# Cross attention's turned keys and weights at other places, and a counter moved where four stages begin

## The chip, the cores and the metric

The kernel runs on one NeuronCore of a Trainium2 chip. TensorE (PE, with its weight loads PEld), VectorE (DVE), ScalarE (ACT), GpSimd (POOL) and SyncE (SP) each work through a queue of their own and wait for each other by semaphores. The metric is the device time of one execution, in microseconds; the times shown are those of several executions, and one more was profiled.

## The reference, cut to what matters

One step of a decoder layer, for two groups that share weights: a prompt of 1024 rows, and eight sample rows that each attend to 8192 cached tokens in pages.

```python
q, k, v, logf, u, z = mixer_inputs(rmsnorm(xp, g_mix), w_in, b_f, g_sgu_v)        # prompt
xp = xp + merge_heads(fox_prompt(q, k, v, logf), sgu_prompt(u, z, w_s, b_s), g_att_out, g_sgu_out, w_o)
mk, mv = memory_kv(mem_prompt, g_mem, w_ck, w_cv)
xp = xp + cross_attend(rmsnorm(xp, g_cross), mk, mv, w_cq, w_co)
f, conv_p = conv_ffn(rmsnorm(xp, g_ffn), zeros, w_up, conv_w, conv_b, w_down);  xp = xp + f
q, k, v, logf, u, z = mixer_inputs(rmsnorm(xs, g_mix), w_in, b_f, g_sgu_v)        # sample: the same layer,
att = fox_sample(q, k, v, logf, cache_k, cache_v, cache_logf, page_table)         # attention over the cache

def cross_attend(xn, mk, mv, w_cq, w_co):        # 4 heads of 256, 256 memory tokens
    q = (xn @ w_cq).reshape(B, T, MEM_HEADS, MEM_HEAD_DIM)
    s = jnp.einsum('bqhd,bmhd->bhqm', q, mk) * (MEM_HEAD_DIM ** -0.5)
    p = jax.nn.softmax(s, axis=-1)
    o = jnp.einsum('bhqm,bmhd->bqhd', p, mv).reshape(B, T, MEM_HEADS * MEM_HEAD_DIM)
    return o @ w_co
```

Outputs are both groups behind a final norm, and the new keys, values, gates and convolution states.

## The kernel before, in words

The prompt is worked through in two halves of 512 rows, as a chain of stages whose names stand in `phase[0]`: `p1` (the input projection), `att0` and `attx` (attention of half 0), `att1` (attention of half 1), `mid0` (merge, output projection and cross attention of half 0), `ffn0`, `mid1`, `ffn1`. Projections are made of three products each (`gemm3`, L272 to L274, or the loops at L1062 to L1064), from weights that SP loads (L249) and ScalarE and VectorE split into a high and a low part (L235, L236).

Cross attention, `cross` (L1137), works on four heads. Its pieces are

- `fetch(h)`: SP loads the head's keys (L1143) and values (L1145);
- `keys(h)`: four transposes on PE (L1170) and a copy on ScalarE (L1174) turn the keys;
- `weigh(h)`: 16 score products in the trace (L1187), a maximum on VectorE (L1189), its scaling (L1192), the exponential (L1195), the reciprocal of the sum on VectorE (L1198), and the scaling of the weights on ScalarE (L1200);
- `turned(h)`: eight transposes (L1207) and two copies (L1208) turn the weights;
- `gather(h)`: the output products (L1215), split by ScalarE and VectorE (L235, L236).

Before these come the query projections, two times four products of 24, in a loop over `n` and `dt_`; `keys(0)`, `keys(1)`, `weigh(0)` and `weigh(1)` stand inside that loop. Behind them stands the output projection. Accumulators in PSUM rotate: four tiles `ba` and two `bb` (`BK`), and the projections, transposes, scores and outputs all draw from these six. Small tiles `t` (seven buffers) hold keys and values.

The sample's work, `sample` (decode, L1371 and on, then `sample_rest`), runs beside the prompt as a list of steps. Each of the 128 key steps gathers four tokens of each half page of cached keys by an indirect DMA that POOL issues (L1425) into one of four tiles `kv`, multiplies by the query and sums on VectorE (L1441 and L1445, in the attention stages L1432 and L1433); value steps gather values (L1486) into the same tiles, in pairs, and PE makes the products (L1492).

What sets the order is a counter. The prompt is a generator that yields its work in units (5.2 for a projection of 24 products, 1 to 4 for a piece of cross attention). Each yield is added to `acc[0]`; while the counter holds at least `PACE` of the stage, a step of the sample's generator is issued and the pace subtracted. In the attention stages a key step is cut into five pieces of 0.2. `held[0]` stops steps between the last output projection of a stage and the end of the next norm; the counter runs on, and the steps are caught up behind it, not more than one yield's worth and one at a time. Once the decode is done, `phase[1]` is `rest` and its pace counts.

The order in which all this is written isn't the last word: `kernel` asks for a planner that lays the written instructions out on a timeline of its own (`schedule_with_timeline_sim`), and gives each engine its queue from that. Some instructions are tied behind others by hand (`behind`, `issue_after`).

Of the kernel before, what the change touches and what calls it, by code (L numbers as in the profile page):

```python
# [73 lines left out]
BKQ = 1  # L74
LA = (2, 2)
PACE = {'p1': 7.0, 'att0': 12.0, 'attx': 26.0, 'mid0': 8.0, 'ffn0': 8.5, 'att1': 11.0, 'mid1': 6.8, 'ffn1': 2.5, 'rest': 2.9}


def build(nc, tc, ctx, a, phases=None):
# [31 lines left out]
    def U(shape, dt=F32):  # L111
        n = 1
        for s in shape[1:]:
            n *= s
        t = upool.tile([P, UW], dt, tag="u", bufs=NU, name=nm("u"))[:, :n]
        if len(shape) == 3:
            t = t.rearrange("p (a b) -> p a b", b=shape[2])
        return t

    def T2(n=512, dt=F32):  # L120
        return tpool.tile([P, 512], dt, tag="t2", bufs=NT, name=nm("t2"))[:, :n]
# [24 lines left out]
    def BK():  # L146
        turn_[0] += 1
        return BB() if turn_[0] % BR == BR - 1 else BA()
# [83 lines left out]
    def split(src, h, l, scale=None):  # L232

        if scale is None:
            nc.scalar.activation(h, src, AF.Copy)  # L235
            nc.vector.tensor_tensor(l, src, h.bitcast(F32), op=ALU.subtract)  # L236
        else:
            nc.scalar.activation(h, src, AF.Copy, scale=scale)
            nc.vector.scalar_tensor_tensor(l, src, scale, h.bitcast(F32), op0=ALU.mult, op1=ALU.subtract)  # L239
# [897 lines left out]
    def cross(xt, sq):  # L1137
        mkn, mkT, mv, pp, pT = ([None] * MH for _ in range(5))

        def fetch(h):  # L1140
            hc = slice(h * MD, (h + 1) * MD)
            mkn[h] = T2().rearrange("p (a b) -> p a b", b=256)
            nc.sync.dma_start(mkn[h], mk_d[:, hc].rearrange("(a p) b -> p a b", p=P))  # L1143
            mv[h] = T2().rearrange("p (a b) -> p a b", b=256)
            nc.sync.dma_start(mv[h], mv_d[:, hc].rearrange("(a p) b -> p a b", p=P))  # L1145
# [20 lines left out]
        def keys(h):  # L1166
            tr = TR()
            for dd in range(2):
                for mt in range(2):
                    nc.tensor.transpose(  # L1170
                        tr[:, dd * 256 + mt * P : dd * 256 + (mt + 1) * P], mkn[h][:, mt, dd * P : (dd + 1) * P], ident
                    )
            mkT[h] = T2().rearrange("p (a b) -> p a b", b=256)
            nc.scalar.activation(mkT[h], tr.rearrange("p (a b) -> p a b", b=256), AF.Copy)  # L1174
# [27 lines left out]
        def turned(h):  # L1202
            pT[h] = U([P, 2, 512])
            for mt in range(2):
                tr = TR()
                for i in range(4):
                    nc.tensor.transpose(tr[:, i * P : (i + 1) * P], pp[h][:, i, mt * P : (mt + 1) * P], ident)  # L1207
                nc.scalar.activation(pT[h][:, mt, :], tr, AF.Copy)  # L1208

        def gather(h):  # L1210
            oh2, ol2 = U([P, 2, 512], F32R), U([P, 2, 512], F32R)
            for dd in range(2):
                ps = BK()
                for mt in range(2):
                    mmul(ps, mv[h][:, mt, dd * P : (dd + 1) * P], pT[h][:, mt, :], start=(mt == 0), stop=(mt == 1))  # L1215
                split(ps, oh2[:, dd, :], ol2[:, dd, :])
                oh.append(oh2[:, dd, :])
                ol.append(ol2[:, dd, :])
# [3 lines left out]
        for n in range(2):  # L1222
            if n:
                ws = [wload(wpair(a["wt_cq"], kk, n * 512, 512), 1024) for kk in range(4)]
            for dt_ in range(4):
# [12 lines left out]
                    fetch(2)  # L1238
                if n and 1 <= dt_ < 3:
                    weigh(dt_ - 1)  # L1240
        keys(2)
        fetch(3)
        turned(0)
        yield 1
        weigh(2)
        yield 3
        gather(0)
        yield 4
        keys(3)
        turned(1)  # L1250
        yield 1
        weigh(3)
        yield 3
        gather(1)
        yield 4
        for h in (2, 3):
            turned(h)
            yield 1
            gather(h)
            yield 4  # L1260
        ys = []
        sq = yield from out_proj(a["wt_co"], oh, ol, xt, ys=ys)
        return ys
# [100 lines left out]
    bgs, acc, phase = [], [0.0], ["p1", None]  # L1364
# [547 lines left out]
    def sample():  # L1912
        yield from decode()
        phase[1] = "rest"
        yield from sample_rest()


    bgs.append(sample())
    seen = 0
    for t in prompt():  # L1920
        ins = nc.cur_bb.bb.instructions
        for e in (ENG.DVE, ENG.PE):
            for i in range(len(ins) - 1, max(seen, len(ins) - 400) - 1, -1):
                if ins[i].engine == e:
                    last[e] = ins[i]
                    break
        if paused[0]:
            t = 0.0
        acc[0] += t
        most = int(t / PACE[phase[1] or phase[0]]) + 1  # L1930
        while bgs and not held[0] and most and acc[0] >= PACE[phase[1] or phase[0]]:
            most -= 1
            acc[0] -= PACE[phase[1] or phase[0]]
            w = next(bgs[0], None)
            if w is None:
                bgs.pop()
            else:
                acc[0] -= (w - 1) * PACE[phase[1] or phase[0]]
        seen = len(nc.cur_bb.bb.instructions)
# [100 lines left out]
```

## Time and profile before

| | us |
|---|---|
| median of 3 runs (lowest to highest) | 1791.92 (1788.94 to 1793.47) |
| the profiled execution | 1793.48 |
| its span | 1791.6 |
| PE busy | 1734.9 (97%) |
| DVE busy | 1401.0 (78%) |
| ACT busy | 733.6 (41%) |
| POOL busy | 483.6 (27%) |

Its mean granted TensorE clock is 0.993 of full speed. By stages, cut at times read from the trace, PE is busy

| stretch, us | stage | PE busy, us | PE idle, us | granted clock |
|---|---|---|---|---|
| 0 to 290 | p1 | 282.25 | 7.75 | 1.00 |
| 290 to 480 | att0, attx, att1 | 169.57 | 20.43 | 0.98 |
| 480 to 694 | mid0 | 208.26 | 5.74 | 0.98 |
| 694 to 1090 | ffn0 | 390.69 | 5.31 | 0.99 |
| 1090 to 1337 | mid1 | 239.79 | 7.21 | 1.00 |
| 1337 to 1791 | ffn1 | 444.34 | 9.66 | 0.99 |

In a row of the order of time stand the start in us, the length in us, the engine, the line, the operation, what it writes and reads by the program's names, the shape, how many instructions are merged in the row, and in brackets how long the engine was idle before it and what ended that.

### The profile page before, as it was taken

To read this page: it belongs to the slowest core of one execution; us is meant where nothing else is said; L and a number is where in the kernel's file an instruction comes from. 1 tells how busy PE (TensorE), PEld (TensorE's weight loads), DVE (VectorE), ACT (ScalarE), POOL (GpSimd) and SP (SyncE) were. 2 spreads that over 40 slices of the span, in tenths; PEclk is the share of its full clock that TensorE was granted. 3 is DMA by queue.
4 is the path that set the end of the run, shared out by engine and by line. 5 is a ranking of instruction groups with operands and counts; after the bars stand their busy time and mean duration, and the time that the engine had idled before them with its cause. 6 is when DMAs were issued, how large, how long until landed. Compare 5 with 4: busy or idle time off the path is not lost.

```text
span 1791.6 us, 25124 instructions
## 1 busy us (share of the span) xinstructions
PE 1734.9 (97%) x9653; PEld 1286.3 (72%) x9653; DVE 1401.0 (78%) x1733; ACT 733.6 (41%) x1374; POOL 483.6 (27%) x461
## 2 busy tenths in 40 slices
PE   8999999889999899999999999999999999999997
PEld 5887776656677667767777777766676778768875
DVE  4789668989788886989999899988885549855344
ACT  6332365466633634433333244235353233333232
POOL 1232334434123332323232132433322122102110
PEclk9999999999999999999999999999999999999999
DMA  8886889787698875778788788988879587568982
GB/s 299 327 287 234 300 306 335 253 290 247 259 390 294 330 272 231 274 281 339 298 291 323 288 308 315 376 308 345 327 288 354 210 306 251 190 260 297 358 311 79
DMA packets 139410, 521.06 MB, mean 291 GB/s; under 512 B 20874, under 2 KB 39818, under 8 KB 106522
## 3 DMA queue, kind: packets, MB, share of 16 engines
q0 software_dynamic: 57168, 341.14, 49.9%
q1 hardware_dynamic: 75210, 165.73, 26.6%
q10 hardware_dynamic: 6912, 12.59, 1.9%
q8 instruction: 76, 1.25, 0.3%
q14 instruction: 44, 0.36, 0.1%
HBM read 495.47 MB, written 23.93 MB: 290 GB/s over the span
## 4 chain that ended last, share of the span: by engine, by line
PE 51%; issue 9%; DMA 9%; DVE 6%; POOL 3%; ACT 2%; POOLq 0%; DVEq 0%; ACTq 0%; SPq 0%
DMA kv<-cache_v,io 6%; PE ba L272 6%; PE ba L274 6%; PE ba L273 6%; PE dv L1492 4%; PE bb L272 3%; PE bb L273 3%; PE bb L274 3%; DMA kv<-cache_k,io 2%; PE ba L1062 1%; PE ba L1063 1%; PE ba L1064 1%; POOL kv L1425 1%; PE dv L331 1%; PE dv L1771 1%
## 5 line engine op out<-in xcount | busy, mean ns | idle before, releaser
L235 ACT ACTIVATE wh<-wr 128x1024 fp32r<-128x1024 f32 (+2 forms) x220 | 228.8, 1044 | 443.2 <-PE ba L273 141.6
L236 DVE TENSOR_TENSOR wl<-wr,wh 128x1024 fp32r<-128x1024 f32 (+2 forms) x220 | 262.9, 1200 | 163.6 <-PE ba L274 58.2
L1425 POOL DMA_INDIRECT kv<-cache_k,io x128 | 182.6, 1427 | 606.8 <-DVE s L1445 308.2
L1441 DVE TENSOR_TENSOR kv<-kv,d 128x1024 f32<-128x1024 f32 (+1 forms) x156 | 258.1, 1681 | 28.4 <-DMA kv<-cache_k,io 25.3
L1445 DVE TENSOR_REDUCE s<-kv 128x16 f32<-128x1024 f32 (+1 forms) x156 | 258.4, 1672 | 0.0
L1486 POOL DMA_INDIRECT kv<-cache_v,io x128 | 161.6, 1262 | 246.8 <-PE dv L1492 163.6
L272 PE MATMUL ba<-u,wh 128*128 128x512 f32 x528 | 209.3, 397 | 0.0
L274 PE MATMUL ba<-u,wl 128*128 128x512 f32 x528 | 209.0, 396 | 0.0
L273 PE MATMUL ba<-u,wh 128*128 128x512 f32 x528 | 208.5, 395 | 0.5 <-DVE u L239 0.5
L272 PE MATMUL ba<-wh,u 128*128 128x512 f32 (+1 forms) x495 | 186.6, 380 | 0.9 <-ACT u L235 0.9
L273 PE MATMUL ba<-wl,u 128*128 128x512 f32 (+1 forms) x495 | 185.1, 375 | 0.0
L274 PE MATMUL ba<-wh,u 128*128 128x512 f32 (+1 forms) x495 | 183.6, 376 | 0.0
L1492 PE MATMUL dv<-kv,s 128*32 128x512 f32 x1024 | 127.1, 598 | 2.0 <-DMA kv<-cache_v,io 2.0
L274 PEld LDWEIGHTS ba<-u,wl 128*128 128x128 f32 x528 | 99.2, 188 | 29.0 <-issue 6.5
L272 PEld LDWEIGHTS ba<-u,wh 128*128 128x128 f32 x528 | 99.3, 188 | 26.4 <-issue 4.8
L273 PEld LDWEIGHTS ba<-u,wh 128*128 128x128 f32 x528 | 99.2, 188 | 25.2 <-issue 2.3
L272 PEld LDWEIGHTS ba<-wh,u 128*128 128x128 f32 x495 | 93.3, 189 | 25.1 <-issue 6.5
L272 PE MATMUL bb<-u,wh 128*128 128x512 f32 x272 | 108.7, 400 | 0.0
L274 PE MATMUL bb<-u,wl 128*128 128x512 f32 x272 | 108.0, 398 | 0.0
L273 PE MATMUL bb<-u,wh 128*128 128x512 f32 x272 | 107.8, 397 | 0.0
L274 PEld LDWEIGHTS ba<-wh,u 128*128 128x128 f32 x495 | 93.1, 188 | 19.6 <-issue 2.5
L273 PEld LDWEIGHTS ba<-wl,u 128*128 128x128 f32 x495 | 93.3, 189 | 18.3 <-issue 1.7
(454 smaller groups left out, 3308.6 us busy)
## 6 DMA issues: line engine op xcount, KB each, us to landing
wr<-w_up SPq DMA_DIRECT2D x88, 512.0 KB
kv<-w_up POOLq DMA_DIRECT2D x22, 1024.0 KB
wr<-wt_down SPq DMA_DIRECT2D x40, 512.0 KB
kv<-w_down POOLq DMA_DIRECT2D x11, 1024.0 KB
wr<-w_in SPq DMA_DIRECT2D x16, 512.0 KB
wr<-wt_o SPq DMA_DIRECT2D x16, 512.0 KB
wr<-wt_cq SPq DMA_DIRECT2D x16, 512.0 KB
wr<-wt_co SPq DMA_DIRECT2D x16, 512.0 KB
```

What stands on the lines that cost most here:

```text
L235: nc.scalar.activation(h, src, AF.Copy)
L236: nc.vector.tensor_tensor(l, src, h.bitcast(F32), op=ALU.subtract)
L272: mmul(out, sh, mh, start=(i == 0), stop=False)
L273: mmul(out, sh, ml, start=False, stop=False)
L274: mmul(out, sl, mh, start=False, stop=(i == n - 1))
L331: mmul(ps[32 * j : 32 * j + 32, :w], xT[:, k, :] if nk == 8 else xT[:, k * 8 : k * 8 + 32], raw[:, q, j * w : (j + 1) * w], start=(k == 0) ...
L1062: mmul(pss[i], mh[k][:, tb], wh, start=(k == korder[0]), stop=False)
L1425: nc.gpsimd.indirect_dma_start(kv, None, a["cache_k"], off(kidx[:, b, ch : ch + 1]))
L1441: nc.vector.tensor_tensor(kvv[:, i : i + m, :], kvv[:, i : i + m, :], qb.unsqueeze(1).broadcast_to((P, m, 512)), op=ALU.mult)
L1445: nc.vector.tensor_reduce(s[:, ch * 4 + i : ch * 4 + i + m, :].rearrange("p k h -> p (k h)"), kvv[:, i : i + m, :].rearrange("p k (h d) -> ...
L1486: nc.gpsimd.indirect_dma_start(kv, None, a["cache_v"], off(kidx[:, b, ch : ch + 1]))
L1492: mmul(dv[32 * j : 32 * j + 32, :], s[:, ch * 4 : ch * 4 + 4, :].rearrange("p k h -> p (k h)"), kvv[:, j, :], start=(ch == 1), stop=(ch == ...
```

## The change: what it does

It has two parts. In `cross`, `keys(2)` and `fetch(3)` move from behind the loop of query projections to before its last projection; `keys(3)` moves from behind `gather(0)` to before it; `turned(2)` moves from behind `gather(1)` to before it, and `turned(3)` from behind `gather(2)` to before it. The units that are yielded stay the same in sum, 26, and two of them change places.

In the loop that issues the sample's steps, the first yield of a stage adds a share of that stage's pace to the counter: -0.1 of 11.0 at `att1`, 0.25 of 8.0 at `mid0`, 0.12 of 8.5 at `ffn0` and 0.4 of 6.8 at `mid1`.

```diff
+CREDIT = {'att1': -0.1, 'mid0': 0.25, 'ffn0': 0.12, 'mid1': 0.4}
...
                 if n and 1 <= dt_ < 3:
                     weigh(dt_ - 1)
-        keys(2)
-        fetch(3)
+                if n and dt_ == 2:
+                    keys(2)
+                    fetch(3)
         turned(0)
         yield 1
         weigh(2)
         yield 3
+        keys(3)
         gather(0)
         yield 4
-        keys(3)
         turned(1)
         yield 1
         weigh(3)
         yield 3
+        turned(2)
+        yield 1
         gather(1)
         yield 4
-        for h in (2, 3):
-            turned(h)
-            yield 1
-            gather(h)
-            yield 4
+        turned(3)
+        yield 1
+        gather(2)
+        yield 4
+        gather(3)
+        yield 4
...
+    entered = []
...
+        if phase[0] not in entered:
+            entered.append(phase[0])
+            acc[0] += CREDIT.get(phase[0], 0.0) * PACE[phase[0]]
         acc[0] += t
```

## The prediction

> **What bounds the kernel now.** I read the page's head first, then the two stretches that the edit of cross attention touches by windows, then the order of time on each engine inside them.
>
> ```profile
> span 1791.6 us, 25124 instructions
> PE 1734.9 (97%) x9653; PEld 1286.3 (72%) x9653; DVE 1401.0 (78%) x1733; ACT 733.6 (41%) x1374; POOL 483.6 (27%) x461
> ...
> 599.50:641.40 41.90, 36.16 (x152) 22.04 (x151) 30.23 (x36) 21.47 (x54) 13.61 (x9) 0.92 0.87 327
> 1238.90:1275.90 37.00, 33.90 (x154) 20.17 (x153) 33.02 (x37) 20.84 (x56) 11.87 (x10) 1.00 0.94 369
> ```
>
> TensorE sets the end: it is idle for 1791.6 - 1734.9 = 56.7 us of the span. So a change that keeps the arithmetic can only win idle time of PE, or time at a reduced clock. The two windows (length, then busy time of PE, PEld, DVE, ACT, POOL, then the granted clock) are the parts of cross attention behind its last query product, half 0 and half 1. PE idles 41.90 - 36.16 = 5.74 us in the first and 37.00 - 33.90 = 3.10 us in the second; the clock is 0.92 in the first. The order of time on PE says where:
>
> ```profile
> 599.53 0.60 PE L1170 MATMUL bb<-cp,t 128*128 128x128 f32 x4
> 599.97 1.04 PE L1207 MATMUL ba<-cp,u 128*128 128x128 f32 x8
> 602.13 1.99 PE L1187 MATMUL bb<-t,u 128*128 128x256 f32 x8 [1.12 <-ACT t L1174]
> ...
> 605.69 1.02 PE L1215 MATMUL ba<-u,t 128*128 128x512 f32 x2
> 606.55 1.02 PE L1215 MATMUL bb<-u,t 128*128 128x512 f32 x2
> 607.50 1.92 PE L1492 MATMUL dv<-kv,s 128*32 128x512 f32 x16
> 609.35 1.12 PE L1215 MATMUL ba<-u,t 128*128 128x512 f32 x2
> ...
> 611.17 0.60 PE L1170 MATMUL ba<-cp,t 128*128 128x128 f32 x4
> ...
> 616.68 6.48 PE L1187 MATMUL ba<-t,u 128*128 128x256 f32 x16 [4.04 <-ACT t L1174]
> ...
> 634.41 1.12 PE L1215 MATMUL ba<-u,t 128*128 128x512 f32 x2 [0.58 <-ACT u L1208]
> ```
>
> ```profile
> 1241.19 3.72 PE L1187 MATMUL ba<-t,u 128*128 128x256 f32 x16 [0.77 <-ACT t L1174]
> ...
> 1252.31 1.99 PE L1187 MATMUL ba<-t,u 128*128 128x256 f32 x8 [0.65 <-ACT t L1174]
> 1254.14 1.89 PE L1187 MATMUL bb<-t,u 128*128 128x256 f32 x8
> 1255.87 3.60 PE L1215 MATMUL ba<-u,t 128*128 128x512 f32 x8
> ...
> 1261.56 1.12 PE L1215 MATMUL ba<-u,t 128*128 128x512 f32 x2 [1.22 <-ACT u L1208]
> ...
> 1268.65 1.12 PE L1215 MATMUL bb<-u,t 128*128 128x512 f32 x2 [0.47 <-ACT u L1208]
> ```
>
> The brackets are all of the idle time: in half 0 1.12 + 4.04 + 0.58 = 5.74, in half 1 0.77 + 0.65 + 1.22 + 0.47 = 3.11. Two kinds: scores (L1187) that wait for the turned keys (the copy L1174), and outputs (L1215) that wait for the turned weights (the copy L1208). Besides, the 16 score products at 616.68 took 6.48 us where the same 16 took 3.72 us at 1241.19: 2.76 us more, at half clock (windows of the same columns):
>
> ```profile
> 311.69:315.10 3.41, 1.28 (x12) 0.96 (x13) 3.35 (x5) 1.06 (x3) 1.69 (x2) 1.00 1.05 353
> 315.10:318.52 3.42, 3.42 (x12) 2.55 (x11) 3.39 (x6) 1.68 (x3) 2.27 (x3) 0.50 0.92 308
> ...
> 612.06:615.47 3.41, 0.59 (x6) 0.35 (x4) 3.41 (x4) 0.83 (x3) 0.00 (x0) 1.00 1.02 422
> 615.47:618.88 3.41, 2.19 (x5) 1.84 (x6) 3.41 (x6) 3.40 (x10) 0.94 (x1) 0.50 1.03 428
> 618.88:622.30 3.42, 3.42 (x9) 2.70 (x9) 3.30 (x4) 2.07 (x8) 0.00 (x0) 0.50 1.03 418
> ```
>
> The long wait has a cause of its own. The next rows are VectorE, then ScalarE, in that place, and the scaled weights of half 1:
>
> ```profile
> 611.64 2.36 DVE L1441 TENSOR_TENSOR kv<-kv,d 128x1024 f32<-128x1024 f32 x2 [3.40 <-DMA kv<-cache_k,io]
> 613.92 0.68 DVE L1189 TENSOR_REDUCE cmx<-ba 128x2 f32<-128x512 f32 x1
> ...
> 614.64 0.48 ACT L1192 ACTIVATE cbs<-cmx,rq 128x1 f32<-128x1 f32 x2 [3.36 <-DVE cmx L1189]
> ...
> 616.04 0.59 ACT L1174 ACTIVATE t<-ba 128x512 f32<-128x512 f32 x1
> ...
> 617.06 0.60 ACT L1208 ACTIVATE u<-ba 128x512 f32<-128x512 f32 x1
> ...
> 618.17 1.71 ACT L1200 ACTIVATE u<-u,cr 128x256 f32<-128x256 f32 x4
> ...
> 1255.41 1.71 ACT L1200 ACTIVATE u<-u,cr 128x256 f32<-128x256 f32 x4 [2.18 <-DVE cr L1198]
> ...
> 1261.90 1.71 ACT L1200 ACTIVATE u<-u,cr 128x256 f32<-128x256 f32 x4
> ```
>
> A decode step's product stood at the head of VectorE and waited 3.40 us for its gathered keys; the maximum of head 2's scores stood behind it; ScalarE waited 3.36 us for that maximum, and the copy of head 3's keys stood behind it in ScalarE's queue. PE waited for the copy.
>
> **The change part by part.** Nothing is removed or added; 16 transposes of keys, 64 of weights and their copies are written at other places, and decode steps are issued at other yields.
>
> (a) Keys of head 2 before the last query product. Its four transposes (599.53, 0.60 us) then have a projection of 24 products between themselves and weigh(2), so the copy is done long before. That takes 1.12 us out of half 0 and 0.77 out of half 1. The fetch of head 3 that goes with them on SP had been issued before this place in half 0, so it wins nothing and passes nothing:
>
> ```profile
> 582.26 0.38 SPq L1143 DMA_DIRECT2D t<-o_mk  x1
> 592.16 0.38 SPq L1145 DMA_DIRECT2D t<-o_mv  x1
> ```
>
> (b) Weights of heads 2 and 3 one gather sooner. Between turned(3) and gather(3) then lies gather(2), 3.60 us of PE as at 1255.87, and between turned(2) and gather(2) at least gather(1); each copy pair of L1208 takes some 1.2 us (two of 0.60). So 0.58, 1.22 and 0.47 go.
>
> (c) Keys of head 3 before gather(0). In half 1 this takes 0.65 away. In half 0 the wait of 4.04 and the slow clock behind it, 4.04 + 2.76 = 6.80 us, go wholly if the copy gets into ScalarE's idle time ahead of the blocked maximum, and not at all if it stays behind it, or if weigh(3) then lacks an accumulator: the six rotating ones are held by head 2's scores, both outputs of gather(0), whose low parts VectorE must still take, and the turned weights of head 1. Bounds 0 and 6.80; I take the middle, 3.4, since the copy has its chance and the accumulators come free only about 617 (617.06).
>
> (d) What is late next: turned(2) now follows weigh(3) and needs head 2's weights scaled. In half 1 these are ready at 1255.41 + 1.71 = 1257.12, while weigh(3), without 0.77 + 0.65, ends at 1254.14 + 1.89 - 1.42 = 1254.61: 2.51 us short. In half 0 they are ready at 618.17 + 1.71 = 619.88 and weigh(3), without 1.12 + 4.04 + 2.76, ends at 616.68 + 6.48 - 7.92 = 615.24: 4.64 us short. Likewise turned(3): in half 1 its weights are scaled at 1261.90 + 1.71 = 1263.61, 7.58 us behind the scores; the transposes of turned(2) (1.04 as at 599.97), gather(1) (3.60) and a group of decode products (1.92 as at 607.50) cover 6.56, so 1.0 is short, and as much in half 0. All together 2.51 + 4.64 + 2.0 = 9.15 us if everything stays in written order (the 4.64 only where the 6.80 of (c) goes: later scores wait for less); the price reaches down to 0 if the planner plays a gather first. It does such things: the outputs at 605.69, 606.55 and 609.35 are in the order first part of both, then second parts, and not as written. I take 1.5, near the lower end.
>
> (e) The counter. The credits are -0.1 x 11.0 = -1.1, 0.25 x 8.0 = +2.0, 0.12 x 8.5 = +1.02 and 0.4 x 6.8 = +2.72 units; none is taken back, so the counter stands at -1.1, +0.9, +1.92, +4.64 from att1, mid0, ffn0, mid1 on. Run by hand over the yields, that puts 55 of the 290 pieces of decode work at another yield: 14 one yield later in att1; in mid0 five sooner and one later; 13 and 14 sooner in ffn0 and mid1, most by one yield (5.2 units in a projection); 8 sooner behind that, one of them by 11. The last piece stays where it is, at the seventh yield from the end, so the tail is not moved. Each moved step takes its gather on POOL, its products and sums on VectorE, and every second one its value products on PE:
>
> ```profile
> L1425 POOL DMA_INDIRECT kv<-cache_k,io x128 | 182.6, 1427 | 606.8 <-DVE s L1445 308.2
> L1441 DVE TENSOR_TENSOR kv<-kv,d 128x1024 f32<-128x1024 f32 (+1 forms) x156 | 258.1, 1681 | 28.4 <-DMA kv<-cache_k,io 25.3
> ...
> L1492 PE MATMUL dv<-kv,s 128*32 128x512 f32 x1024 | 127.1, 598 | 2.0 <-DMA kv<-cache_v,io 2.0
> ```
>
> Their counts stay, so their work costs the same; what can change are waits. A gather starts when a tile comes free (308.2 us of POOL's waits are for the sums of an earlier step), so a step written sooner does not get its keys sooner by as much, and its product may wait longer on VectorE. Bounds: -2.0, if PE's one wait for gathered values goes, and +6.80, one more event like that of half 0. I take 0: steps moved both ways, and VectorE's waits of 25.3 us reach PE only where PE waits for VectorE.
>
> **Sum**: -(1.12 + 0.77) - (0.58 + 1.22 + 0.47) - 0.65 - 3.4 + 1.5 + 0 = -6.7 us. From the profiled execution, 1793.48 (span 1791.6 and 1.9 around it), this makes 1786.8; that execution lies 1.6 above the median of the runs, so against the median it is 1791.92 - 6.7 = 1785.2. The six small waits of (a) to (c) are 4.81 of it. The ends: -4.81 - 6.80 - 2.0 = -13.6, and with the 6.80 left where it is, the rest of (d) whole and one new event, -4.81 + 2.51 + 2.0 + 6.80 = +6.5.
>
> On the clock, this trace halves it in a stretch that follows one with PE busy 0.59 or 1.28 us of 3.41. The Trainium skill, "TensorE: Matmul & The Clock Gate" (Part 1: The HAM clock gate), has the clock fall after at least one idle window of about 3.4 us. By that rule a wait cut below 3.4 us would already save the 2.76; by the rows, 2.13 us idle of a window (311.69) were enough to lose it, so I count it with the wait.
>
> **The rivals.** First, *the wait only moves*. In the rows above ScalarE and VectorE take their work strictly in order, and a sooner transpose on PE helps only if its copy is also ahead of the blocked instruction. Then the small waits go (-4.81), the 6.80 stays, and (d) costs what is short in half 1, 2.51 + 1.0: -1.3 us, 1790.6. For it: the copy at 616.04 was data-ready at 611.8 and stood behind 614.64. Against it: in half 1 the same queue let it through with 0.65. The same page of the Trainium skill (table at its head) calls the queues of ScalarE and VectorE strict FIFO; the trace agrees with its 3.36 us.
>
> Second, *slower: a step issued sooner holds VectorE in cross attention*. Steps 121 to 124, counted from 0, stand one or two yields sooner in half 1; step 122 now stands ahead of weigh(3), where it stood behind gather(1), while turned(3) needs the maxima of weigh(3) sooner. If their products wait for keys as the one at 611.64 did, each event costs 6.80 us. One is paid by the small waits (-4.81 + 6.80 = +2.0, no change that shows); it decides from the second on: -4.81 + 2 x 6.80 = +8.8 with half 0's own event left as it is, 1800.7. For it: 25.3 us of such waits now. Against it: step 52 is a yield sooner in half 0, which frees its tile sooner for the gather of step 54, the late one.
>
> Third, *the edit does little*, since the planner orders by its own timeline and had put the fetch of head 3 at 582.26 already: then perhaps the two waits for head 2's keys go, 1.12 + 0.77 = 1.9: 1790.0.
>
> **How the numbers follow.** A change of 0.3%, 5.4 us, is about what a measurement tells from none here. Forecast (-3.5 to -13.6 us): 0.50, of it 0.41 beyond 5.4 and 0.09 within. The wait moves: 0.20, of it 0.03 faster, 0.16 same, 0.01 slower. Slower by steps: 0.20, of it 0.18 slower and 0.02 same. Little done: 0.10, 0.01 faster, 0.08 same, 0.01 slower. Faster 0.45, same 0.35, slower 0.20. The range goes to within 1 us of both ends of the sum, -13.6 and +6.5, and leaves out about half of the slower case: 1779 to 1798. The forecast's own range is 1778 to 1788.
>
> **What would show it.** Right: no wait for L1174 before L1187 in either half, none for L1208 before L1215; the two windows together shorter by some 7 us; the granted clock 1.00 in half 0's. A wait of L1207 for the scaling L1200 is the price (d). Wrong in (c): PE still idle 3 us or more before weigh(3) in half 0, with a product of a decode step ahead of a maximum on VectorE. Wrong in (e): new waits of PE outside the two windows that add to over 3 us, or VectorE's waits for gathered keys grown well over 25.3 us.

## The result, and the profile after

The changed kernel takes 1785.36 us (median of 10 runs, 1783.59 to 1794.45); the kernel before took 1793.01 beside it (10 runs, 1787.65 to 1798.91). The ratio is 0.996, with a 95% interval of 0.9945 to 0.9975, so some 7 us are gained. Ratios leave out executions far above the fastest of their kernel; there was one, of 8507.89 us, in the kernel with the steps held in half 1. The forecast was 1785.2. Its total came true. Its sum did not, as the stages and the runs below show: the new order was to bring all of the 6.7 us and the counter nothing, and on the chip neither is shown to win anything alone.

In the names of the code, cross attention's lines, the norm's and the helpers' stand one further down than before (in cross attention the turned keys' copy is L1175, scores L1188, scaled weights L1201, turned weights L1208 and L1209, outputs L1216), and the decode's five further (gathers L1430 and L1491, product L1446, sum L1450, value product L1497).

The head of the page after, and its rows for the decode's products on VectorE and on PE:

```profile
span 1786.4 us, 25125 instructions
...
PE 1733.5 (97%) x9653; PEld 1283.0 (72%) x9653; DVE 1398.2 (78%) x1733; ACT 731.7 (41%) x1374; POOL 494.5 (28%) x461
...
L1446 DVE TENSOR_TENSOR kv<-kv,d 128x1024 f32<-128x1024 f32 (+1 forms) x156 | 258.2, 1681 | 26.4 <-DMA kv<-cache_k,io 25.5
...
L1497 PE MATMUL dv<-kv,s 128*32 128x512 f32 x1024 | 127.3, 599 | 0.1
```

PE is busy for 1.4 us less than before (1733.5 for 1734.9) and idle for 52.9 us in place of 56.7. VectorE's waits for gathered keys are what they were (25.5 for 25.3). PE's wait for gathered values is gone (0.1 for 2.0).

To see where the time goes, three stretches do: up to the first transposes of cross attention's norm in half 0 (I call the stretch A), from there to the same place in half 1 (B: cross attention of half 0, the feed-forward stage, merge of half 1), and from there to the end (C). The kernel before, by windows of these stretches (start and end, length, busy time of PE, PEld, DVE, ACT and POOL, granted clock):

```profile
0.00:515.70 515.70, 487.51 (x2814) 366.57 (x2815) 405.09 (x561) 256.50 (x491) 161.55 (x172) 0.99 0.81 291
515.70:1155.90 640.20, 628.61 (x3040) 466.75 (x3038) 578.62 (x601) 246.61 (x440) 195.18 (x141) 0.99 0.81 304
1155.90:1791.60 635.70, 618.76 (x3803) 453.02 (x3801) 417.25 (x572) 230.52 (x443) 126.88 (x148) 1.00 0.75 277
```

The same three of the changed kernel, and the two parts of cross attention behind the last query product:

```profile
0.00:517.37 517.37, 487.96 (x2814) 365.98 (x2814) 404.78 (x561) 256.34 (x491) 168.26 (x172) 1.00 0.81 289
517.37:1147.40 630.03, 625.07 (x3043) 463.97 (x3042) 580.41 (x603) 245.68 (x440) 192.42 (x141) 1.00 0.83 313
1147.40:1786.39 638.99, 620.46 (x3799) 453.06 (x3797) 413.04 (x570) 229.69 (x443) 133.78 (x148) 0.99 0.74 273
...
601.00:641.00 40.00, 38.28 (x172) 23.48 (x171) 36.03 (x43) 23.32 (x57) 11.09 (x9) 1.00 0.93 359
1236.50:1272.00 35.50, 28.54 (x118) 15.23 (x116) 26.97 (x34) 18.72 (x51) 9.44 (x10) 0.90 0.78 291
```

B is 10 us shorter and C 3 us longer than in this one profile of before; with two more profiles of it, below, that becomes 7 and 2. In half 0's cross attention PE idles 40.00 - 38.28 = 1.72 us, where it idled 5.74, and the clock is 1.00. In half 1's it idles 35.50 - 28.54 = 6.96 us, where it idled 3.11, at a clock of 0.90. The order of time on PE has all of half 0's waits:

```profile
621.94 2.10 PE L1216 MATMUL bb<-u,t 128*128 128x512 f32 x4 [0.58 <-ACT u L1209]
624.61 0.44 PE L1208 MATMUL ba<-cp,u 128*128 128x128 f32 x2 [0.56 <-ACT u L1201]
...
630.00 1.12 PE L1216 MATMUL ba<-u,t 128*128 128x512 f32 x2 [0.58 <-ACT u L1209]
```

The waits for the turned keys are gone, as forecast; the price (d), a wait for scaled weights, is 0.56 us. Half 1 looks otherwise, here on all engines:

```profile
1239.37 1.99 PE L1188 MATMUL bb<-t,u 128*128 128x256 f32 x8 [0.52 <-ACT t L1175]
...
1242.83 1.12 PE L1216 MATMUL bb<-u,t 128*128 128x512 f32 x2 [1.03 <-ACT u L1209]
...
1245.70 2.36 DVE L1446 TENSOR_TENSOR kv<-kv,d 128x1024 f32<-128x1024 f32 x2 [3.28 <-DMA kv<-cache_k,io]
...
1250.30 0.68 DVE L1190 TENSOR_REDUCE cmx<-bb 128x2 f32<-128x512 f32 x1
...
1251.02 0.48 ACT L1193 ACTIVATE cbs<-cmx,rq 128x1 f32<-128x1 f32 x2 [7.21 <-DVE cmx L1190]
1251.40 1.69 ACT L1201 ACTIVATE u<-u,cr 128x256 f32<-128x256 f32 x4
1251.95 0.69 PE L1208 MATMUL ba<-cp,u 128*128 128x128 f32 x2 [5.41 <-ACT u L1201]
...
1252.43 3.62 PE L1216 MATMUL ba<-u,t 128*128 128x512 f32 x4
```

A key step's product waits 3.28 us for its keys at the head of VectorE. Behind it stand two low parts of outputs, half of the step's sums and then the maximum of the next scores (1250.30); ScalarE waits 7.21 us for that maximum, and the scaling of head 2's weights stands behind it; PE, which now has head 2's transposes ahead of the rest of gather(1) (1252.43), waits 5.41 us for the scaling. It is the event that half 0 showed before, in the other half, and the forecast had both halves of it as prices: (d), and the one event of its second rival. The granted clock by windows of 3.41 us of the changed kernel shows what it costs beside the wait:

```profile
1245.75:1249.16 3.41, 0.79 (x2) 0.00 (x0) 3.41 (x4) 0.00 (x0) 0.00 (x0) 1.00 1.02 430
1249.16:1252.57 3.41, 0.62 (x3) 0.62 (x4) 3.41 (x6) 1.55 (x5) 0.13 (x1) 0.50 0.49 207
1252.57:1255.99 3.42, 3.42 (x6) 1.25 (x5) 0.51 (x3) 3.17 (x13) 0.82 (x1) 0.50 0.48 139
```

(0.62 + 3.42) / 2 = 2.0 us of work are lost at half clock.

### The profile page after: what moved, and what is told of

Its sections match the earlier page's. It is cut to its first block, busy times and chain, and to the rows that moved or that the text cites. A ratio compares the mean times of both kernels' runs of the same rounds, so it can differ in the third digit from the quotient of the medians.

```text
span 1786.4 us, 25125 instructions
## 1 busy us (share of the span) xinstructions
PE 1733.5 (97%) x9653; PEld 1283.0 (72%) x9653; DVE 1398.2 (78%) x1733; ACT 731.7 (41%) x1374; POOL 494.5 (28%) x461
## 3 DMA queue, kind: packets, MB, share of 16 engines
q8 instruction: 76, 1.25, 0.3%
## 4 chain that ended last, share of the span: by engine, by line
PE 59%; issue 7%; DVE 6%; DMA 5%; ACT 1%; POOL 1%; POOLq 0%; DVEq 0%; ACTq 0%
PE ba L273 9%; PE ba L275 8%; PE ba L274 8%; PE dv L1497 5%; PE bb L273 4%; PE bb L275 4%; PE bb L274 4%; DMA kv<-cache_k,io 3%; PE dv L332 1%; PE dv L1776 1%; DMA kv<-cache_v,io 1%; PE ba L1063 1%; PE ba L1065 1%; DMA kv<-cmv 1%; PE ba L1064 1%
## 5 line engine op out<-in xcount | busy, mean ns | idle before, releaser
L1430 POOL DMA_INDIRECT kv<-cache_k,io x128 | 183.3, 1432 | 594.0 <-DVE s L1450 308.9
L1446 DVE TENSOR_TENSOR kv<-kv,d 128x1024 f32<-128x1024 f32 (+1 forms) x156 | 258.2, 1681 | 26.4 <-DMA kv<-cache_k,io 25.5
L1450 DVE TENSOR_REDUCE s<-kv 128x16 f32<-128x1024 f32 (+1 forms) x156 | 258.5, 1673 | 0.0
L1491 POOL DMA_INDIRECT kv<-cache_v,io x128 | 161.7, 1264 | 240.8 <-PE dv L1497 165.5
L1497 PE MATMUL dv<-kv,s 128*32 128x512 f32 x1024 | 127.3, 599 | 0.1
```

The source lines that it names most:

```text
L1430: nc.gpsimd.indirect_dma_start(kv, None, a["cache_k"], off(kidx[:, b, ch : ch + 1]))
L1446: nc.vector.tensor_tensor(kvv[:, i : i + m, :], kvv[:, i : i + m, :], qb.unsqueeze(1).broadcast_to((P, m, 512)), op=ALU.mult)
L1450: nc.vector.tensor_reduce(s[:, ch * 4 + i : ch * 4 + i + m, :].rearrange("p k h -> p (k h)"), kvv[:, i : i + m, :].rearrange("p k (h d) -> ...
L1491: nc.gpsimd.indirect_dma_start(kv, None, a["cache_v"], off(kidx[:, b, ch : ch + 1]))
L1497: mmul(dv[32 * j : 32 * j + 32, :], s[:, ch * 4 : ch * 4 + 4, :].rearrange("p k h -> p (k h)"), kvv[:, j, :], start=(ch == 1), stop=(ch == ...
```

## The experiments

Two comparisons come first, since the others are read by them.

**The same kernel again.** The kernel before was profiled twice more.

> The kernel before, profiled a second time: how far a stage's length moves from execution to execution with the same instructions. The stretch to the first norm of cross attention was 515.7 us in the first profile and 521.1 in the kernel with the new order alone, whose queues are the same up to there; if that is chance, some stretch moves here by 2 us or more. The stretch with cross attention of half 0 (164.5) and that of half 1 (163.2) should come back within 2 us, or the comparison of single profiles says nothing.

> The kernel before, a third profile. If the wait of 4.04 us and the half clock behind it in half 0's cross attention belong to its queues, they are there again (two of three profiles); if they are chance of one execution, the wait is 1.5 us or less as in the second profile.

The second took 1794.48 us, the third 1790.05. Their waits of PE for turned keys in half 0, the second's from its order of time on PE:

```profile
603.92 1.99 PE L1187 MATMUL bb<-t,u 128*128 128x256 f32 x8 [0.39 <-ACT t L1174]
...
615.94 3.72 PE L1187 MATMUL ba<-t,u 128*128 128x256 f32 x16 [1.50 <-ACT t L1174]
```

and the third's, with its stretches by windows:

```profile
602.12 1.99 PE L1187 MATMUL bb<-t,u 128*128 128x256 f32 x8 [0.75 <-ACT t L1174]
...
613.30 3.72 PE L1187 MATMUL ba<-t,u 128*128 128x256 f32 x16 [0.66 <-ACT t L1174]
...
0.00:516.01 516.01, 486.07 (x2813) 365.30 (x2814) 407.17 (x563) 256.54 (x491) 170.58 (x172) 1.00 0.81 291
516.01:1150.36 634.35, 625.22 (x3040) 463.95 (x3039) 575.90 (x598) 246.12 (x440) 186.66 (x141) 1.00 0.82 307
1150.36:1788.01 637.65, 620.64 (x3803) 454.34 (x3801) 416.63 (x572) 230.42 (x443) 130.63 (x148) 0.99 0.75 276
```

The wait of 4.04 us with the half clock behind it, 6.80 us in all, was there in one execution of three. In the others the same place waits 1.50 and 0.66 us, and the 16 score products take their 3.72. The order of the instructions is the same each time; the decode's product that waited 3.40 us for its keys in the first profile waits 0.24 us in the second and not at all in the third. So what looked like a property of the order was a chance, seen once in three, and the waits are worth (6.80 + 1.50 + 0.66) / 3 = 3.0 us on average.

The second profile also misses its own expectation. The stretches of the two cross attentions, from norm to norm, were to come back within 2 us, or single profiles say nothing; they came to 159.2 us for 164.5 in half 0 and to 165.3 for 163.2 in half 1. So differences of 2 to 5 us between two single profiles prove nothing by themselves, and what follows leans on the timed runs and on what several profiles share.

The stretches of every kernel that was profiled, made as above, with the ratios of the timed runs:

| kernel | A | B | C | ratio to before (95%) |
|---|---|---|---|---|
| before | 515.7, 518.2, 516.0 | 640.2, 636.3, 634.4 | 635.7, 637.8, 637.7 | |
| changed | 517.4 | 630.0 | 639.0 | 0.996 (0.9945 to 0.9975) |
| new order alone (two profiles) | 521.1, 523.6 | 634.3, 633.8 | 644.9, 640.8 | 1.0014 (1.0000 to 1.0028) |
| credits alone | 515.4 | 634.8 | 641.5 | 1.0002 (0.9982 to 1.0023) |
| changed, without mid1's credit | 518.8 | 630.4 | 639.3 | 0.9973 (0.9956 to 0.9991) |
| changed, credits of att1 and mid0 alone | 523.4 | 631.0 | 634.7 | 0.9974 (0.9954 to 0.9994) |
| changed, credit of mid0 alone | 515.9 | 633.4 | 641.7 | 1.0028 (1.0008 to 1.0049) |
| changed, weights turned late in half 1 | 520.0 | 630.3 | 639.8 | 0.9981 (0.9961 to 1.0002) |
| changed, steps held in half 1 | 519.3 | 630.4 | 637.7 | 0.9969 (0.9957 to 0.9982) |
| the same with the old order | 517.9 | 635.0 | 641.7 | 1.0018 (1.0000 to 1.0035) |
| changed, steps held sooner in half 1 | 515.9 | 629.9 | 658.8 | 1.0081 (1.0051 to 1.0112) |

A is no part of the change but for one of the four credits, and it scatters by 8 us. The new order alone has the same instructions in the same order on every engine as the kernel before up to half 0's cross attention, and its A is 521.1 and 523.6 beside 515.7 to 518.2. So I read B and C. Their means before are 637.0 and 637.1. B parts the kernels well: in the six profiles that have the new order with the credits of att1 and mid0 it is 629.9 to 631.0, in the eight others 633.4 to 640.2.

**The order alone and the credits alone.**

```
 new order alone, from the changed kernel        credits alone, from the kernel before
-CREDIT = {'att1': -0.1, 'mid0': 0.25, ...}      +CREDIT = {'att1': -0.1, 'mid0': 0.25, ...}
+CREDIT = {}                                     +        acc[0] += CREDIT.get(phase[0], 0.0) * PACE[phase[0]]
```

> The new order in cross attention, all four credits left out. A, the forecast's split (the order brings all, the credits nothing): about -6.7 us against before, ratio 0.996, and PE's wait before weigh(3) in half 0 shrinks to 3 us or less. B, the split that the changed kernel's trace suggests (its half 0 is rid of the decode product that held VectorE because step 52 is issued a yield sooner by the credit of mid0): without credits that product waits again, the small waits of 4.8 us go but the 6.8 us stay: -1 to -3 us, ratio 0.9985 or more. C, the planner's order of everything shifts and decides: stalls in other places than in either kernel, time anywhere within 7 us of before.

> All four credits, cross attention in the old order. A: nothing, ratio 1.000, within 2 us. B: the wait of 4.04 us in half 0 and its half clock (6.8 us) go, the small waits (4.8) stay, and half 1 gets the wait that the changed kernel shows there (5.41 us before the transposes of weights): -4 to +2 us. C: as above, within 7 us of before.

> The new order without credits, profiled a second time. If the order is what half 0 gains and half 1 loses, half 0's stretch comes back at 157 to 160 us (before 164.5) and half 1's at 166 to 169 (before 163.2), with the wait for an accumulator or for VectorE near weigh(3) in half 1 again. If it was chance, either comes back nearer to the kernel before.

The order alone gives 1.0014, the credits alone 1.0002, both together 0.996. 1793 x (0.996 - 1.0014) = -9.7 us lie between the order with its credits and without. The order alone wins 2.9 us in B (mean 634.0 for 637.0) and loses 5.8 in C (642.8 for 637.1). Theory A of the first expectation falls by that; theory B has the ratio, but not its reason, since the event of 6.80 us is in neither profile of the order alone. For the credits alone, theory A holds.

A second profile of the order alone (1799.95 us) was to tell whether the loss in C is chance as half 0's event was. Part of it is: in half 1 the first profile has PE waiting 3.29 us at the scores (1256.03), behind a decode product that waited 4.10 us for its keys, with a half clock of 3.41 us after it. The second has neither, and half 1 from norm to norm takes 165.4 us there for 168.1 in the first. The rest of the loss is in both. Its place is the norm of the last feed-forward stage; there the first profile of the order alone has waits of 1.17, 1.20 and 0.58 us, and the second has, by the order of time on PE and the windows of the clock:

```profile
1328.80 0.51 PE L1082 MATMUL bb<-wl,u 128*128 128x512 f32 x1
1329.14 0.39 PE L1083 MATMUL bb<-wh,u 128*128 128x512 f32 x1
...
1331.04 0.39 PE L281 MATMUL ba<-u,wh 128*128 128x256 f32 x1 [1.16 <-ACT u L239]
...
1332.99 0.33 PE L1124 MATMUL ba<-cp,u 128*128 128x128 f32 x1 [1.21 <-DVE u L240]
...
1333.96 0.58 PE L281 MATMUL ba<-u,wh 128*128 128x256 f32 x1 [0.39 <-ACT u L239]
...
1341.38 0.38 PE L281 MATMUL ba<-u,wh 128*128 128x256 f32 x1 [0.58 <-ACT u L239]
...
1330.43:1333.85 3.42, 1.32 (x7) 0.97 (x7) 2.94 (x10) 3.42 (x10) 0.00 (x0) 1.00 1.02 406
1333.85:1337.26 3.41, 3.30 (x14) 3.05 (x15) 3.41 (x8) 1.70 (x6) 0.56 (x1) 0.50 0.76 306
```

The waits make 3.34 us and the half clock 3.30 / 2 = 1.65, 5.0 together. In the three profiles of the kernel before, the waits of this norm add to 1.4 to 1.7 us at full clock, so the order alone costs some 3.5 us there, about what the second profile's C lies above 637.1. Two products of the output projection (L1082, L1083) are all that is left between the norm's transposes and the feed-forward products (L281); then PE has only the chain of transpose, gain (L239, L240) and product, and waits at each step of it.

In the changed kernel, with the four credits, these waits and the half clock are gone. A second gain of the credits lies in B, from the norm of `ffn0` to the norm of half 1's cross attention. The windows are the second profile of the order alone, then the changed kernel:

```profile
680.98:1157.42 476.44, 470.71 (x2245) 351.95 (x2243) 441.04 (x432) 175.23 (x282) 143.50 (x103) 0.99 0.80 303
...
674.62:1147.40 472.78, 469.70 (x2251) 352.15 (x2250) 439.50 (x431) 175.86 (x285) 142.55 (x103) 1.00 0.82 309
```

PE idles 5.73 us in the one (5.49 in the first profile of the order alone) and 3.08 in the other, and the half clock at `ffn0`'s norm lasts 6.83 us in both profiles of the order alone and 3.41 in the changed kernel. Half 0's cross attention up to that norm takes the same, 157.9 and 157.4 us beside 157.3. So this part of the gain is not in cross attention at all.

**Which credit.** All runs of this group have the new order; the diffs change one line.

```
-CREDIT = {'att1': -0.1, 'mid0': 0.25, 'ffn0': 0.12, 'mid1': 0.4}
+CREDIT = {'att1': -0.1, 'mid0': 0.25, 'ffn0': 0.12}     # without mid1's
+CREDIT = {'mid0': 0.25}                                 # mid0's alone
+CREDIT = {'att1': -0.1, 'mid0': 0.25}                   # att1's and mid0's
```

> The changed kernel without the credit of mid1 (0.4 of 6.8 units). In the changed kernel PE waits 5.41 us in half 1's cross attention, with 6.8 us at half clock behind it, while a decode product waits 3.28 us for its keys on VectorE. If the credit's sooner steps make that event, it is gone here: 5 to 8 us faster than the changed kernel, ratio to before 0.992 or less, granted clock 1.00 around 1250 us. If the new order of the weights' transposes makes it, it stays and the time is that of the changed kernel, ratio 0.996.

> The changed kernel with the credit of mid0 alone (0.25); those of att1, ffn0 and mid1 left out. Theory A (the gain lies in where steps stand in half 0's cross attention and the norm behind it): the 2.8 us at the norm of ffn0 stay, the wait for gathered values near 782 us comes back with 1 to 2 us, and the half clock at the norm of ffn1 comes back with 3 to 5 us, so the ratio is 0.998 to 1.001. Theory B (any credit that shifts the steps is enough): ratio 0.995 to 0.997 as in the changed kernel. Theory C (mid0's credit is not it): the norm of ffn0 shows 6.8 us at half clock or waits as in the kernel before, and the ratio is 1.000 to 1.003 as with the new order alone.

> The changed kernel with the credits of att1 (-0.1) and mid0 (0.25) alone, so that the counter stands at +0.9 units from half 0's cross attention on; those of ffn0 and mid1 left out. It lies between the kernel with mid0's credit alone (1.0028, cross attention and output projection of half 0 161.6 us) and the one without mid1's credit (0.9973, 157.3 us). Theory A (att1's tenth counts, since with it the steps in half 0's cross attention are those of the changed kernel): that stage comes to 157 to 158 us, and the ratio is 0.996 to 0.999. Theory B (ffn0's credit counts): the stage comes to 157 to 158 us too, but the feed-forward stage behind it to 475 us or more in place of 473, or the wait for gathered values near 782 us is back, and the ratio is 1.000 to 1.004. Theory C (no single credit; where steps happen to meet): the stage itself stays at 160 us or more.

Without mid1's credit the ratio is 0.9973, without ffn0's too it is 0.9974; both intervals hold the changed kernel's 0.996, so what these two credits bring is not resolved. Without both, PE's wait for gathered values is back, with 1.30 us at 782.13 (2.03 in the first profile of before, 0.91 in the second of the order alone). It isn't ffn0's credit as such that removes it: in the profiles with the new order the wait is gone where the counter stands at +1.92 or +2.0 units there, with mid0's credit alone too, and it is there at 0 and at +0.9.

With mid0's credit alone it is 1.0028, slower than before. The credit of att1, a tenth of a step taken away, is thus worth 0.54% or 9.7 us on top of mid0's: the two intervals don't meet. The profiles agree: B + C are 1275.1 without and 1265.7 with it. That is theory A of the last run: from norm to norm, half 0's cross attention takes 157.1 us, where 157 to 158 were expected, and 161.6 with mid0's credit alone. Most of those 4.5 us is moved work, though: with mid0's credit alone 143 products of the output projection stand ahead of that norm's transposes, and 121 with both credits, as in the changed kernel. Neither att1's credit without mid0's was tried nor a mid0 credit that sets the counter to +0.9 by itself, so whether the tenth in att1 counts, or the counter's level behind it, stays open. Of the run with mid0's alone, theory A has one part right: the waits at the last norm are there again, with 1.16, 1.21 and 0.58 us. The wait for gathered values isn't, and the ratio is the one that theory C gave, so mid0's credit by itself earns nothing on top of the new order. In the kernel with the two credits, the order of time on PE in that norm reads:

```profile
1321.30 0.50 PE L1082 MATMUL ba<-wl,u 128*128 128x512 f32 x1
...
1323.72 0.39 PE L1083 MATMUL bb<-wh,u 128*128 128x512 f32 x1
...
1324.09 0.36 PE L281 MATMUL ba<-u,wh 128*128 128x256 f32 x1
...
1326.24 0.39 PE L281 MATMUL ba<-u,wh 128*128 128x256 f32 x1 [0.27 <-ACT u L239]
```

From 1321.30 to 1323.72 run eleven products of the output projection, between the value products of the decode and the feed-forward's first product. In the order alone there were two, in the kernel before four, without a wait for a gain over 0.2 us; so their number alone does not decide. While they run, the gains are made, and the longest wait for one is 0.27 us. The products are the same in number; the planner placed more of them behind the transposes. Why its timeline does so for a tenth of a step in a stage over 800 us ahead I have not followed; it stays open.

**What holds half 1's cross attention.** Three runs were to take the 5.41 us away. The first puts the turned weights of half 1 back to their old places; the second and third set the hold of the steps in half 1's cross attention, the second behind the query products with the new order and with the old one, the third ahead of the query products.

```
 weights turned late in half 1        steps held in half 1               steps held sooner
+        if phase[0] == "mid0":       +        held[0] = phase[0] == "mid1"   +        held[0] = phase[0] == "mid1"
             turned(2)                         turned(0)                               for n in range(2):
             gather(1)  ...                    ...                                     ...
+        else:                        +        held[0] = False                +        held[0] = False
+            gather(1)                         ys = []                                 ys = []
+            turned(2)  ...
```

> The changed kernel, but in half 1 the transposes of the weights of heads 2 and 3 stand where they stood before (behind gather(1) and gather(2)). If the sooner transposes make half 1's wait of 5.41 us (they stand in PE's queue ahead of products of gather(1) that were ready), 2 to 7 us of it go: ratio to before 0.992 to 0.995. If the decode product on VectorE makes it whatever stands there, PE still waits 3 us or more in that place and the time is that of the changed kernel, ratio 0.996.

> The changed kernel, with the decode's steps held back in half 1 from behind the last query product of cross attention to its output projection, and caught up from there. D, VectorE's decode work is what half 1's cross attention waits for, so a sooner transpose only moves the wait: with the steps away PE's waits from weigh(2) to the last gather in half 1 fall from 7 us to under 2.5 us, no half clock there, and the stretch of half 1 from norm to norm is 4 us or more shorter than the changed kernel's 164.5; the held steps cost part of it later: ratio to before 0.990 to 0.995. E, the new order itself is bad for half 1: its waits stay at 5 us or more, ratio 0.996 or higher.

> The same hold with all four credits, but cross attention in the old order in both halves. If with VectorE free the new order is worth what it is in half 0 (some 7 us there and 3 in half 1), this is 6 to 10 us slower than the one with the new order, ratio to before 0.998 to 1.001, with waits of the scores for the turned keys still there in both halves. If the order is worth nothing without the steps, the two are equal within 2 us.

> The changed kernel, but in half 1 no decode step is issued from before the loop of the query products of cross attention until its output projection; the steps follow later, so the work is all done. Theory (steps on VectorE hold half 1): the first hold began too late, since the catch-up steps that hold the maximum were issued inside the query loop; with them out of the way PE's waits in half 1's cross attention fall from 7.3 to under 3 us and its stage from 164.5 to about 160, as half 0's 157; the steps left over are done behind it, so the time is 1780 to 1788 if the tail takes them without a wait (ratio 0.990 to 0.996). Rival (the new order itself is short by what scaling the weights takes): a wait of 3 to 6 us before the weights' transposes stays in half 1, and the ratio is 0.996 or more. Rival 2: TensorE lacks its filling work there, the waits grow to over 10 us, ratio over 1.000.

Weights turned late: the wait of 5.41 us goes and waits of 1.56, 1.45, 1.25 and 1.73 us come in its place, with PE idle for 7.8 us between the first transposes of half 1's two norms (cross attention's and the feed-forward's), where the changed kernel has 7.5. There is no half clock in this stretch. The ratio is 0.9981, which is neither of the two that were expected; the interval overlaps with the changed kernel's. So, as far as one profile of each tells, the place of the turned weights decides where PE waits in half 1, not for how long.

Steps held: with the new order a wait of 5.28 us for the scaled weights stays, as theory E had it, and all 40 key products are still between half 1's norms, as in the changed kernel. The hold begins behind the query loop and so stopped none of them. With the old order the ratio is 1.0018, 8.4 us more by the medians, and the intervals don't meet: under the same credits the new order is again worth about half a per cent.

In half 1 the wait is not a chance of one landing. The decode's product waits 3.28 us for its keys in the changed kernel, 2.58 without mid1's credit (PE then 3.63 for the scaled weights), 3.08 with the weights turned late and 3.15 with the steps held. Without ffn0's and mid1's credits it waits 0.29 and PE 0.12, at full clock, and half 1 from norm to norm takes 158.9 us for 164.5; that is one profile. In the order alone such a product waits 4.10 us in one profile and not in the other. So the event is not the order's by itself; ffn0's credit seems to bring it, which no run by itself shows.

Steps held sooner: only 24 of 40 key products and 96 of 160 value products are left between the two norms. That stretch is 155.2 us in place of 164.5, 9.3 us shorter, but 64 value products at 1.92 / 16 us each are 7.7 us of work that only moved. A wait stays, in the order of time on all engines of this run (the decode's lines two further down):

```profile
1239.43 2.36 DVE L1448 TENSOR_TENSOR kv<-kv,d 128x1024 f32<-128x1024 f32 x2 [2.47 <-DMA kv<-cache_k,io]
...
1241.71 2.34 DVE L1452 TENSOR_REDUCE s<-kv 128x16 f32<-128x1024 f32 x2
...
1243.96 0.17 DVE L1199 RECIPROCAL cr<-cl 128x4 f32<-128x4 f32 x1
...
1244.16 1.70 ACT L1201 ACTIVATE u<-u,cr 128x256 f32<-128x256 f32 x4 [1.27 <-DVE cr L1199]
...
1244.73 0.47 PE L1208 MATMUL ba<-cp,u 128*128 128x128 f32 x1 [4.64 <-ACT u L1201]
```

One product that was issued sooner still waits 2.47 us there; its sums stand ahead of the reciprocal that the scaling needs. Then the work that was put off has less cover behind: C grows to 658.8 us, with waits of PE that add to 17.4 us behind the second norm (1.6 in the changed kernel), and the ratio is 1.0081. The theory that a hold of the steps frees half 1 falls as a remedy, and the first rival's wait of 3 to 6 us is there; that a key step on VectorE is the link is what both traces show. A half 1 with no step in it at all was not tried.

No kernel of the series is shown to beat the changed one.

## Why the prediction was right, and where it was not

**The total** was right by steps that were wrong in both directions: -6.7 was forecast, 0.4% or 7.2 us were measured, and the sum had it as -6.7 for the order and 0 for the counter. Measured are +2.5 (1.0014) for the order alone and -9.7 for the credits on top of it.

**(a), (b), (c) in half 0**: the waits for turned keys went, and the clock in the window came to 1.00. The 6.80 us event was put down as fixed, with 3.4 as the middle of what might be won; it was there in one profile of three. All of half 0's waits and the lost clock make 1.12 + 6.80 + 0.58 = 8.5, 0.39 + 1.50 + 0.65 + 0.58 = 3.1 and 0.75 + 0.66 + 1.04 + 0.58 = 3.0 us in the three (0.65 and 1.04 are for gathered values), 4.9 on average; in the order alone they make 2.4 and 2.0, in the changed kernel 1.72. The order wins 2.7 there, where the sum had 1.12 + 0.58 + 3.4 = 5.1. The outputs still wait for turned weights in the changed kernel, with two of 0.58 (b).

**(a), (b), (c) in half 1, and (d)**: the four waits, 3.11 us in all, were to go. Waits of 0.52, 1.03 and 5.41 came, and 2.0 at half clock. (d) was mis-sized: 1.5 was taken for both halves of a bound of 9.15, "near the lower end", since the planner may play a gather first. It did so in half 0 of the changed kernel (0.56 us); in the order alone the price is all that half 0 waits, 2.4 and 2.0 us. The bound itself counts half 1 twice: once turned(2) has waited until 1257.12, the cover of 6.56 us reaches 1263.68, past the 1263.61 at which the next weights are scaled, so the further 1.0 is not short. In half 1 of the changed kernel the planner put one part of the gather behind the transposes that waited. The single event of the second rival is the cause: a product that waits for keys, ahead of a maximum. What the sum lacked is that both come together: the later the scaling, the more stands behind it in the new order. (Of the transposes of weights 32 move, two heads in two halves, not 64; no term hangs on that.)

**(e)** failed. The term was taken as 0 from bounds of -2.0 and +6.80; the credits are worth about -9.7 on top of the new order and nothing on the old one. The -2.0, PE's wait for gathered values, came true. The rest lies outside the bounds, since they were made from what a moved step does to the wait beside it. In the runs, the place of steps also changes where the planner puts the output projection's products, and with that goes whether the last norm has cover (5.0 us in the order alone; the same waits in its other profile and with mid0's credit alone, and none of them in the changed kernel, without mid1's credit, or with the two credits, where waits of 0.8 to 1.2 us are left). The second place is the stretch behind `ffn0`'s norm, 3.6 us shorter with the credits. "Steps moved both ways" was an argument for a mean of zero, not for a small effect. The sign named for a wrong (e), new waits of PE over 3 us outside the two windows, looked for a loss alone: it came in the order without credits, not in the changed kernel.

**The rivals.** "The wait only moves" is what half 1 shows, with another wait than it named. "Slower by steps" had the mechanism, a product ahead of a maximum, once and not twice. "The edit does little" was wrong for the edit as a whole, but near for each of its parts alone: 1.0014 and 1.0002 lie within 0.3% of no change.

That the total came out within 0.2 us is luck: the errors of the terms cancel.

## What to carry to other kernels

An order written out and a pace at which other work is let in are one edit where a planner fills the gaps: cost them together, and try each alone before either is credited. A wait that comes from the landing of an indirect DMA can be a chance and not a term (in half 0 of the kernel before it was long once in three profiles; in half 1 it was there in the changed kernel and in each of three of its variants); profile the same kernel twice before 4 us of it go into a sum. When work is moved about, look at the next chain with little beside it (here the last norm), because that is where the cover it gave is missed.

## What the runs showed of the hardware

The clock is not lost by the share of idle time alone. By windows of 3.41 us of the kernel before:

```profile
693.98:697.39 3.41, 1.81 (x12) 1.16 (x10) 2.66 (x5) 2.30 (x7) 0.57 (x1) 1.00 1.00 422
697.39:700.81 3.42, 1.94 (x8) 1.65 (x9) 1.16 (x3) 3.39 (x10) 0.55 (x1) 0.50 1.02 425
...
782.71:786.13 3.42, 1.83 (x16) 0.42 (x16) 1.79 (x3) 1.17 (x2) 0.46 (x1) 1.00 0.97 344
786.13:789.54 3.41, 3.41 (x19) 2.78 (x16) 0.61 (x1) 0.00 (x0) 2.36 (x3) 1.00 0.77 273
...
1178.71:1182.12 3.41, 1.71 (x13) 1.39 (x13) 3.41 (x8) 1.33 (x3) 0.17 (x1) 1.00 1.02 401
1182.12:1185.54 3.42, 3.42 (x18) 2.85 (x17) 3.36 (x6) 0.00 (x0) 1.02 (x2) 1.00 0.20 81
```

PE busy 1.81 us of one was followed by half clock, 1.83 and 1.71 were not; at the last norm of the order alone 1.32 was. Over all fourteen profiles, the first and last 12 us left aside, the windows at full clock part like this: each of the 45 with PE busy up to 1.50 us was followed by half clock, 15 of the 69 with 1.51 to 2.08 us were, and none of the 7033 with more. What decides between is not known. So in these traces some 1.9 us or more of idle time within one window was always followed by half clock in the next, which costs up to 1.7 us more; less idle time may or may not be. The Trainium skill, "TensorE: Matmul & The Clock Gate" (Part 1: The HAM clock gate), has the clock fall after at least one idle window of about 3.4 us. The windows' length agrees, and two wholly idle ones, in the runs with the steps held, were followed by half clock; but a window need not be wholly idle (0.79, 1.32 and 1.81 us busy in the rows shown).

And the same order of instructions up to half 0's cross attention took from 515.7 to 523.6 us in five executions of two kernels. PE's idle time there (28.2 to 32.9 us) and what it lost at half clock (1.7 to 7.8 us) are the whole of it: without them the five lie between 483.7 and 485.0 us. Why the waits differ isn't known; the scatter is as large as the effect under study, and only the timed runs in number tell 0.4% from it.
